# Summing 32,768 float32 rows into one: casting loads and a float16 fold, against float32 loads and a hand-written ring

## The chip, the cores and the metric

The kernel runs on one core of one Trainium2 chip. The metric is device time in microseconds (us) of one execution; of the kernel before, three runs gave a median of 629.18 us (629.15 to 629.20).

## The reference

```python
def reference(grad_output):            # [32, 1024, 2048] float32
    return np.sum(grad_output, axis=(0, 1)).astype(np.float32)
```

The input is 32,768 rows of 2048 float32 numbers, 268.4 MB. The result is the column sum: 2048 numbers, 8 KB. Every byte of the input has to come from HBM into the core's SBUF once.

## The kernel before, in words

The 32,768 rows are 256 "row blocks" of 128 rows, one row for each SBUF partition. A load takes m row blocks at a time: partition p gets m consecutive rows, so it reads m x 8 KB of consecutive bytes. A plan (a Python list, built before anything is recorded) names for each load the first row, m, the type it has in SBUF, the engine whose queue issues it, and the columns. In order:

- two loads of one row block each, kept as float32, issued on SP's queue (`PRE_TILES`);
- 30 loads of eight row blocks each (4 MB in SBUF), then one of four, two of two: issued on GpSimd's queue into float16 tiles, so that the transfer itself casts;
- five loads of one row block, float16;
- the last row block as four loads of 512 columns each, float16, last columns first.

All of it goes through one loop (lines 132 to 168). Line 146 issues the load. If the tile is float16 and has several rows a partition, VectorE adds its second half to its first in float16 (line 152), which halves what TensorE has to do. TensorE then multiplies a column of ones (the weights, `lhsT`, 128x1) with 512 columns at a time (line 161): the product is one row of 512 column sums over the 128 partitions, accumulated in one of four PSUM banks, `psum0` to `psum3`, one bank for each 512 columns. At the end ScalarE and VectorE copy two banks each to `res` (lines 175 and 177) and SP's queue writes `res` out (line 178).

The order of instructions is that of the loop; the tile framework puts in the waits. The eight-row tiles live in a pool of three buffers (`T_BUFS`), so a load waits until VectorE has added the tile three loads earlier.

Of the kernel before, what the change touches and what calls it, by code (L numbers as in the profile page):

```python
# [1 line left out]

# [4 lines left out]

P = 128
MM_N = 512  # L10

PRE_TILES = 2
PRE_M = 1
PRE_ENGS = ("sync", "sync")
BULK_M = 8
BULK_TAPER = (4, 2)
USE_DVE = True
TAIL_TILES = 5
COL_SPLIT_LAST = True
T_BUFS = 3  # L20
C_BUFS = 3
TAIL_BUFS = 8
BULK_ENGS = ("gpsimd",)
OUT_COPY_ENGS = ("scalar", "vector")


@with_exitstack
def kernel(
    ctx: ExitStack,
    tc: tile.TileContext,  # L30
    grad_output: bass.AP,
    out: bass.AP,
):
    nc = tc.nc
    fp32 = mybir.dt.float32
    fp16 = mybir.dt.float16

    D = out.shape[-1]
    flat = grad_output.rearrange("b s d -> (b s) d")
    R = flat.shape[0]  # L40
    assert R % P == 0 and D % MM_N == 0
    nbanks = D // MM_N
    n_row_blocks = R // P

    pre_tiles = min(PRE_TILES, n_row_blocks // PRE_M // 4)
    col_split = COL_SPLIT_LAST and nbanks > 1
    taper = [m for m in BULK_TAPER if m < BULK_M]
    n_small = TAIL_TILES + (1 if col_split else 0)
    while pre_tiles * PRE_M + sum(taper) + n_small > n_row_blocks:
        if TAIL_TILES and n_small > 1:  # L50
            n_small -= 1
        elif taper:
            taper = taper[1:]
        else:
            col_split = False
            n_small = min(n_small, 1)
            break
    n_tail = n_small - (1 if col_split else 0)

    plan: list = []  # L60
    row = 0
    for i in range(pre_tiles):
        plan.append((row, PRE_M, fp32, PRE_ENGS[i % len(PRE_ENGS)], 0, D))
        row += P * PRE_M
    tail_start = R - P * (n_small + sum(taper))
    bi = 0
    while row < tail_start:
        take = min(P * BULK_M, tail_start - row)
        plan.append((row, take // P, fp16, BULK_ENGS[bi % len(BULK_ENGS)], 0, D))
        bi += 1  # L70
        row += take
    for m in taper:
        plan.append((row, m, fp16, BULK_ENGS[bi % len(BULK_ENGS)], 0, D))
        bi += 1
        row += P * m
    for _ in range(n_tail):
        plan.append((row, 1, fp16, BULK_ENGS[bi % len(BULK_ENGS)], 0, D))
        bi += 1
        row += P
    if col_split:  # L80
        for b in range(nbanks - 1, -1, -1):
            plan.append((row, 1, fp16, BULK_ENGS[bi % len(BULK_ENGS)], b * MM_N, MM_N))
            bi += 1
        row += P
    assert row == R

    io_pool = ctx.enter_context(tc.tile_pool(name="io", bufs=T_BUFS))
    pre_pool = None
    if pre_tiles:
        pre_pool = ctx.enter_context(tc.tile_pool(name="pre", bufs=pre_tiles))  # L90
    c_pool = None
    if USE_DVE:
        c_pool = ctx.enter_context(tc.tile_pool(name="csum", bufs=C_BUFS))
    n_small_tiles = n_tail + (nbanks if col_split else 0)
    tail_pool = None
    if n_small_tiles:
        tail_pool = ctx.enter_context(
            tc.tile_pool(name="tail", bufs=min(n_small_tiles, TAIL_BUFS))
        )
    const_pool = ctx.enter_context(tc.tile_pool(name="const", bufs=1))  # L100
    psum_pool = ctx.enter_context(tc.tile_pool(name="psum", bufs=1, space=bass.MemoryType.PSUM))

    ones16 = const_pool.tile([P, 1], fp16)
    nc.vector.memset(ones16[:], 1.0)  # L104
    ones32 = None
    if pre_tiles:
        ones32 = const_pool.tile([P, 1], fp32)
        nc.vector.memset(ones32[:], 1.0)  # L108

    accs = [  # L110
        psum_pool.tile([1, MM_N], fp32, tag=f"psum{b}", name=f"psum{b}")
        for b in range(nbanks)
    ]
    res = const_pool.tile([1, D], fp32)

    def uses_dve(entry) -> bool:
        _, m, dt_, _, _, col_n = entry
        return USE_DVE and dt_ is fp16 and m > 1 and col_n == D

    def n_chunks(entry) -> int:  # L120
        _, m, dt_, _, _, col_n = entry
        n = (m * col_n) // MM_N
        return n // 2 if uses_dve(entry) else n

    total_mm = [0] * nbanks
    for e in plan:
        for j in range(n_chunks(e)):
            total_mm[((e[4] + j * MM_N) % D) // MM_N] += 1
    started = [False] * nbanks
    n_mm = [0] * nbanks  # L130

    for i, entry in enumerate(plan):
        row0, m, dt_, eng_name, col_lo, col_n = entry
        rows = flat[row0 : row0 + m * P]
        if col_n == D:
            src = rows.rearrange("(p m) d -> p (m d)", p=P)
        else:
            src = rows[:, col_lo : col_lo + col_n]

        if dt_ is fp16:  # L140
            big = m > 1 and col_n == D
            pool, tag = (io_pool, "T") if big else (tail_pool, "Ttail")
            T = pool.tile([P, m * col_n], fp16, tag=tag, name=f"t{i}")
        else:
            T = pre_pool.tile([P, m * col_n], fp32, tag="Tpre", name=f"t{i}")
        getattr(nc, eng_name).dma_start(out=T[:], in_=src)  # L146

        red = T
        if uses_dve(entry):
            half = (m * col_n) // 2  # L150
            C = c_pool.tile([P, half], fp16, tag="C", name=f"c{i}")
            nc.vector.tensor_tensor(  # L152
                out=C[:], in0=T[:, :half], in1=T[:, half:], op=mybir.AluOpType.add
            )
            red = C

        w = ones16 if dt_ is fp16 else ones32
        for j in range(n_chunks(entry)):
            b = ((col_lo + j * MM_N) % D) // MM_N
            n_mm[b] += 1  # L160
            nc.tensor.matmul(  # L161
                accs[b][:, :],
                lhsT=w[:],
                rhs=red[:, j * MM_N : (j + 1) * MM_N],
                start=(not started[b]),
                stop=(n_mm[b] == total_mm[b]),
            )
            started[b] = True

    bank_order = list(range(nbanks - 1, -1, -1)) if col_split else list(range(nbanks))  # L170
    for k, b in enumerate(bank_order):
        eng = OUT_COPY_ENGS[k % len(OUT_COPY_ENGS)]
        dst = res[:, b * MM_N : (b + 1) * MM_N]
        if eng == "scalar":
            nc.scalar.copy(out=dst, in_=accs[b][:, :])  # L175
        else:
            nc.vector.tensor_copy(out=dst, in_=accs[b][:, :])  # L177
    nc.sync.dma_start(out=out[None, :], in_=res[:])


# [1 line left out]
_INS = ['grad_output']  # L182
_OUTS = [((2048,), 'float32')]


# [23 lines left out]
```

## Time and profile before

| what | value |
|---|---|
| median of three runs | 629.18 us |
| span of the profiled execution, first to last instruction | 627.2 us |
| mean granted TensorE clock (1 is full speed) | 0.65 |
| casting loads of eight row blocks, 4096 KB each in SBUF | 30 |
| median time of one of them from issue to landing | 53.1 us |
| two float32 loads, 1024 KB each, issue to landing | 14.3 us |
| output, bytes | 8.0 KB |

The page counts the DMA's bytes and GB/s as they are written into SBUF; a casting load reads twice what it writes. "Busy" of an engine is the share of the span in which it runs an instruction; time in a queue or a wait is not counted. PE is TensorE's matmuls and PEld its weight loads, DVE is VectorE, ACT ScalarE, POOL GpSimd and SP the sync engine. A float32 matmul of the program appears as two records, and so do its weight loads: eight matmuls of the two float32 tiles are sixteen records. In the chain that ended last, "another core or an unknown queue" stands for a wait on a load that had been issued more than 50 us earlier. The time between the span and the run's time lies before the first and after the last instruction.

### The profile page before, as it was taken

The page shows a single profiled execution, that of the slowest core. Times are in us where ns is not written, and L with a number is a line of the kernel's source. Part 1 is how long each engine was busy: PE and PEld are TensorE (multiplying, and loading weights), DVE is VectorE, ACT ScalarE, POOL GpSimd, SP SyncE. Part 2 cuts the span into 40 slices and gives each one's busy share as a digit, 9 for nine tenths or more (in the row PEclk, how much of TensorE's full clock was granted, in tenths as well). Part 3 has the DMA queues.
Part 4 walks back from the last instruction along what each step waited for, and adds up shares of the span by engine and source line. Part 5 has one row for each costly group of instructions (what it writes and reads, how often), then busy time and mean ns, then how long its engine had stood idle before and what let it go on. Part 6 is the DMA issues. An engine that isn't in the chain of part 4 may idle for free.

```text
span 627.2 us, 1267 instructions
## 1 busy us (share of the span) xinstructions
PE 195.1 (31%) x536; PEld 58.1 (9%) x536; DVE 138.9 (22%) x37; ACT 2.4 (0%) x3; POOL 22.6 (4%) x46
## 2 busy tenths in 40 slices
PE   3323320333203333123341134321333312343165
PEld 0001100011000111001110011100111000111011
DVE  0202222022220122211222202222022221122320
ACT  0000000000000000000000000000000000000000
POOL 1000000000000000000000000000000000000110
PEclk9677556775567665667655776656676567665677
DMA  9999999999999999999999999999999999999997
GB/s 242 226 234 201 234 201 234 202 232 203 232 203 232 203 232 203 232 204 230 205 230 205 230 205 230 205 230 206 228 207 228 207 224 211 224 211 221 206 206 139
DMA packets 6344, 135.36 MB, mean 216 GB/s; under 512 B 705, under 2 KB 1217, under 8 KB 1857
## 3 DMA queue, kind: packets, MB, share of 16 engines
q0 software_dynamic: 6048, 133.17, 98.9%
q1 hardware_dynamic: 290, 2.11, 0.9%
q8 instruction: 4, 0.07, 0.0%
q14 instruction: 2, 0.02, 0.0%
HBM read 268.44 MB, written 0.01 MB: 428 GB/s over the span
## 4 chain that ended last, share of the span: by engine, by line
another core or an unknown queue 66%; DVE 21%; DMA 11%; PE 1%; POOL 1%; issue 0%; DVEq 0%; POOLq 0%
DVE c L152 20%; DMA t<-in_grad_output_dram 11%; PE psum L161 1%; POOL t L146 1%; DVEq L152 0%; DVE res L177 0%; POOLq L193 0%
## 5 line engine op out<-in xcount | busy, mean ns | idle before, releaser
L161 PE MATMUL psum<-c,ones 128*1 128x512 f16 x496 | 175.9, 533 | 405.5 <-DVE c L152 405.5
L152 DVE TENSOR_TENSOR c<-t 128x8192 f16<-128x8192 f16 (+2 forms) x33 | 137.5, 4167 | 471.1 <-DMA t<-in_grad_output_dram 471.1
L161 PEld LDWEIGHTS <-ones 128*1 128x1 f16 x520 | 56.5, 109 | 537.5 <-issue 516.4
L146 POOL DMA_DIRECT2D t<-in_grad_output_dram x42 | 22.4, 538 | 590.4 <-DVE c L152 575.3
L161 PE MATMUL psum<-t,ones 128*1 128x512 f16 (+1 forms) x40 | 19.4, 639 | 23.5 <-DMA t<-in_grad_output_dram 23.5
L177 DVE COPY res<-psum 1x512 f32<-1x512 f32 x2 | 1.4, 679 | 13.9 <-PE psum L161 13.9
L161 PEld LDWEIGHTS psum<-t,ones 128*1 128x1 f32 x16 | 1.6, 106 | 27.5 <-DMA t<-in_grad_output_dram 14.1
L175 ACT COPY res<-psum 1x512 f32<-1x512 f32 x2 | 1.1, 575 | 621.1 <-PE psum L161 621.1
L175 ACT ACT_TABLE_LOAD x1 | 1.3, 1283 | 0.7 <-PEq L193 0.7
L104 DVE MEMSET ones<- 128x1 f16 x1 | 0.1, 59 | 0.8 <-PEq L193 0.8
L193 POOL MEMSET const-float32-0.0<- 128x1 f32 x1 | 0.1, 100 | 0.2 <-issue 0.2
L193 POOL MEMSET const-bfloat16-1.0<- 128x1 bf16 x1 | 0.1, 103 | 0.0
L193 POOL MEMSET const-float32-1.0<- 128x1 f32 x1 | 0.1, 100 | 0.0
L193 POOL MEMSET const-uint8-127<- 128x1 uint8 x1 | 0.1, 100 | 0.0
L108 DVE MEMSET ones<- 128x1 f32 x1 | 0.1, 59 | 0.0
## 6 DMA issues: line engine op xcount, KB each, us to landing
t<-in_grad_output_dram POOLq DMA_DIRECT2D x30, 4096.0 KB, 53.1
t<-in_grad_output_dram POOLq DMA_DIRECT2D x5, 512.0 KB, 20.4
t<-in_grad_output_dram SPq DMA_DIRECT2D x2, 1024.0 KB, 14.3
t<-in_grad_output_dram POOLq DMA_DIRECT2D x2, 1024.0 KB, 26.6
t<-in_grad_output_dram POOLq DMA_DIRECT2D x1, 2048.0 KB, 29.0
t<-in_grad_output_dram POOLq DMA_DIRECT2D x4, 128.0 KB, 16.1
out_dram<-res SPq DMA_DIRECT2D x1, 8.0 KB
```

What stands on the lines that cost most here:

```text
L104: nc.vector.memset(ones16[:], 1.0)
L108: nc.vector.memset(ones32[:], 1.0)
L146: getattr(nc, eng_name).dma_start(out=T[:], in_=src)
L152: nc.vector.tensor_tensor(out=C[:], in0=T[:, :half], in1=T[:, half:], op=mybir.AluOpType.add)
L161: nc.tensor.matmul(accs[b][:, :], lhsT=w[:], rhs=red[:, j * MM_N : (j + 1) * MM_N], start=(not started[b]), stop=(n_mm[b] == total_mm[b]),)
L175: nc.scalar.copy(out=dst, in_=accs[b][:, :])
L177: nc.vector.tensor_copy(out=dst, in_=accs[b][:, :])
L193: nc = _bacc.Bacc("TRN2", target_bir_lowering=False, num_devices=1)
```

## The change

The kernel is written anew, with the waits set by hand (semaphores, `wait_ge`) in one block that the tile framework does not reorder.

- **Loads.** All loads are float32 and are issued on SP's queue. One buffer, `ring`, has three slots of eight rows a partition (3 x 64 KB a partition). 30 loads of eight row blocks go round the three slots; then come loads of 6, 4, 3 and 2 row blocks and the last row block in two pieces, columns 0 to 1663 and 1664 to 2047. Load i waits for `s_vec >= 2(i-2)`, that is for the first add of tile i-2, the last instruction that reads the slot.
- **VectorE.** The running sum is four rows a partition, 8192 numbers, held in the first half of the newest slot. For each load there are two float32 adds of 128x8192: the running sum of the slot before is added to the second half, then the second half to the first. Each add waits for the one before it by semaphore.
- **TensorE.** It does nothing until VectorE has finished the 30th tile. Then it sums the four running rows and the 16 late rows in float32, four matmuls of 512 columns for each row. The four go to four column groups of the array (`tile_position` 0, 32, 64, 96) and so to four partitions of a single PSUM bank.
- **End.** One copy by VectorE of that bank (128x512), one output DMA of four rows of 2 KB from partitions 0, 32, 64 and 96.

The core of the new code (`W` is 16384 numbers, a slot's width; `H` half of it; `Q` is 512):

```diff
-        getattr(nc, eng_name).dma_start(out=T[:], in_=src)
...
+        q = nc.sync
+        for i in range(VEC_TILES):
+            s = i % SLOTS
+            if i >= SLOTS:
+                q.wait_ge(s_vec, 2 * (i - 2))
+            src = flat[i * W // D * P : (i + 1) * W // D * P].rearrange("(p m) d -> p (m d)", p=P)
+            q.dma_start(out=ring[:, s * W : (s + 1) * W], in_=src).then_inc(landed[s], 16)
+        waited = 0
+        for k, (r0, m, c0, w, at) in enumerate(loads):
+            need = 2 * (VEC_TILES - 2) if (at + m * w - 1) // W == VEC_TILES % SLOTS else 2 * (VEC_TILES - 1)
+            if need > waited:
+                q.wait_ge(s_vec, need)
+                waited = need
...
+            q.dma_start(out=ring[:, at : at + m * w], in_=src).then_inc(late[k], 16)
...
-            nc.vector.tensor_tensor(
-                out=C[:], in0=T[:, :half], in1=T[:, half:], op=mybir.AluOpType.add
-            )
...
+        for i in range(VEC_TILES):
+            s = i % SLOTS
+            lo = ring[:, s * W : s * W + H]
+            hi = ring[:, s * W + H : (s + 1) * W]
+            v.wait_ge(landed[s], 16 * (i // SLOTS + 1))
+            if i:
+                b = ((i - 1) % SLOTS) * W
+                v.wait_ge(s_vec, 2 * i - 1)
+                v.tensor_tensor(out=hi, in0=hi, in1=ring[:, b : b + H], op=add).then_inc(s_vec, 1)
+                v.wait_ge(s_vec, 2 * i)
+            v.tensor_tensor(out=lo, in0=lo, in1=hi, op=add).then_inc(s_vec, 1)
...
+        def rows(at, w, c0, first, last):
+            for g in range(4):
+                lo, hi = max(c0, g * Q), min(c0 + w, (g + 1) * Q)
+                if lo >= hi:
+                    continue
+                yield t.matmul(
+                    acc[32 * g : 32 * g + 1, lo - g * Q : hi - g * Q],
+                    lhsT=ones[:],
+                    rhs=ring[:, at + lo - c0 : at + hi - c0],
+                    start=first,
+                    stop=last,
+                    tile_position=(0, 32 * g),
+                    skip_group_check=True,
+                )
+        t.wait_ge(s_one, 2)
+        t.wait_ge(s_vec, 2 * VEC_TILES - 1)
+        base = ((VEC_TILES - 1) % SLOTS) * W
+        for j in range(TILE_ROWS // 2):
+            for _ in rows(base + j * D, D, 0, j == 0, False):
+                pass
+        for k, (r0, m, c0, w, at) in enumerate(loads):
+            t.wait_ge(late[k], 16)
+            for j in range(m):
+                mm = list(rows(at + j * w, w, c0, False, k == len(loads) - 1))
+        mm[-1].then_inc(s_pe, 1)
...
+        a.wait_ge(s_pe, 1)
+        a.tensor_copy(out=res[:], in_=acc[:, :Q]).then_inc(s_res, 1)
+        q.wait_ge(s_res, 1)
+        q.dma_start(
+            out=out.rearrange("(g c) -> g c", g=4), in_=res[0:97:32, :]
+        ).then_inc(s_out, 16)
+        q.wait_ge(s_out, 16)
```

## The prediction

> **What bounds the kernel now.** I read the page's busy shares first, then the DMA queues, then the chain that ended last, and only then the groups of instructions.
>
> ```profile
> PE 195.1 (31%) x536; PEld 58.1 (9%) x536; DVE 138.9 (22%) x37; ACT 2.4 (0%) x3; POOL 22.6 (4%) x46
> ...
> DMA  9999999999999999999999999999999999999997
> ...
> q0 software_dynamic: 6048, 133.17, 98.9%
> q1 hardware_dynamic: 290, 2.11, 0.9%
> ...
> HBM read 268.44 MB, written 0.01 MB: 428 GB/s over the span
> ```
>
> No compute engine is busy for a third of the span, while the 16 DMA engines are full in all slices but the last. Queue q0 writes 133.17 MB because its loads turn float32 into float16; what it reads is twice that. In a stretch of the steady stage (100 to 293 us):
>
> ```profile
> DMA packets 1440, 41.91 MB, mean 217 GB/s; under 512 B 160, under 2 KB 160, under 8 KB 160
> ```
>
> 217 GB/s written is 434 GB/s read. The waits of VectorE give the same rate: its adds start at 66.06, 85.51 and 104.81 us, and the shortest step, 19.30 us, is one load of 8.39 MB read. So the kernel is a stream of 268.4 MB with a short head and a tail, and only what changes the stream's rate, its head or its tail counts. The end of the chain:
>
> ```profile
> 596.21 24.26 DMA t<-in_grad_output_dram
> 620.48 0.04 issue
> 620.52 3.59 PE psum L161 x8
> 624.10 0.02 issue
> 624.13 0.68 DVE res L177
> ```
>
> The reader is to see that the end hangs on the last loads, then on eight matmuls and one copy. The output DMA is issued at 624.90 and the span ends at 627.16, so it costs 2.26 us. The span is 2.0 us under the median of the runs (629.18); I keep these 2.0 us as a constant around it.
>
> **1. The stream: same bytes read, twice the bytes written.** All loads move from GpSimd's queue to SP's and land as float32. The question is whether a transfer that writes as much as it reads keeps 434 GB/s. The trace has one: the two first loads on q1, before q0 starts to move data (3 to 5.5 us):
>
> ```profile
> DMA packets 145, 1.06 MB, mean 423 GB/s; under 512 B 16, under 2 KB 16, under 8 KB 16
> ...
> q1 hardware_dynamic: 145, 1.06, 100.2%
> ```
>
> The engines are full and 423 GB/s are written and read. That is 2.5% under the 434 of q0, but these rows are 8 KB long, q0's rows are 64 KB. The loads of q0 that also have 8 KB rows (one row a partition) start their matmuls at 613.11, 615.58, 618.02 and 620.52 us: 2.47 us for 1.05 MB is 425 GB/s. So 8 KB rows give the same rate by either queue and with either width written; what differs is the row's length. The changed kernel loads 64 KB rows. Bounds: 268.4 MB at 423 GB/s is 634.5 us (every row as dear as an 8 KB row), at 19.30 us a load 32 x 19.30 = 617.6 us. I take 19.31, 618.0 us, from the rows of the same length, and 0.4 us for the last short pieces.
>
> **2. Do the loads stay back to back?** The new wait: load i waits on SP for the first add of tile i-2; behind it stand all later loads and the output DMA, and VectorE waits for those. That add starts when tile i-2 has landed and lasts some 8.7 us (below), while tile i-1 takes 19.3 us; load i is thus issued 10.6 us before it is needed. SP's issue took 0.40 us, and 1.9 us passed from its first issue (0.74) to steady packets. The cover is 10.6 - 2.3 = 8.3 us, so the wait costs nothing. GpSimd's 42 issues (22.4 us) vanish; they were hidden.
>
> **3. VectorE: two float32 adds of 8192 elements a load.** Not in the trace. The nearest rows:
>
> ```profile
> L152 DVE TENSOR_TENSOR c<-t 128x8192 f16<-128x8192 f16 x30 | 132.8, 4425 | 459.7 <-DMA t<-in_grad_output_dram 459.7
> ...
> L152 DVE TENSOR_TENSOR c<-t 128x2048 f16<-128x2048 f16 x2 | 2.5, 1226 | 3.0 <-DMA t<-in_grad_output_dram 3.0
> ...
> L177 DVE COPY res<-psum 1x512 f32<-1x512 f32 x2 | 1.4, 679 | 13.9 <-PE psum L161 13.9
> ```
>
> Float16: (4425 - 1226) / 6144 = 0.52 ns an element and 160 ns fixed. Bounds for float32: no dearer, 4.43 us; or the copy's whole 679 / 512 = 1.33 ns an element, 10.9 us. Taking the fixed 160 ns off the copy gives 1.01 ns, twice the float16 price, as twice the bytes would: 8.5 to 8.7 us. I take 8.7. Two adds, each with a semaphore step of 0.13 us (0.03 + 0.05 + 0.05 before an add in the chain), are 17.7 us a load, under the 19.3 of the load: hidden, 1.6 us to spare. The Trainium skill (VectorE: DVE Perf Modes, the section on the TRN2 errata) gives a float32 add of two tensors as (N + 151) / 0.96 ns, an estimate of 8.69 us here; no row of this trace shows it.
>
> **4. The last 16 rows, where the risk lies.** The 30th load lands at 2.45 + 0.25 + 30 x 19.31 = 582.0 us (head: step 5). VectorE's adds end at 599.7. Only then may TensorE start, on 4 running rows and on 16 late rows, of which six have already landed and the last lands at 621.1. A row of 2048 columns is four float32 matmuls. Their price:
>
> ```profile
> 27.57 0.13 PEld L161 LDWEIGHTS psum<-t,ones 128*1 128x1 f32 x1 [0.73 <-issue]
> 28.16 0.09 PEld L161 LDWEIGHTS psum<-t,ones 128*1 128x1 f32 x1 [0.47 <-issue]
> 28.59 0.08 PEld L161 LDWEIGHTS psum<-t,ones 128*1 128x1 f32 x1 [0.34 <-issue]
> 29.02 0.08 PEld L161 LDWEIGHTS psum<-t,ones 128*1 128x1 f32 x1 [0.34 <-issue]
> ```
>
> A matmul shows as two weight loads and two passes. A pass takes 0.43 us (28.59 to 29.02) once the clock is up and 0.855 us before (25.86 to 26.71); in this burst the clock came up after some 3 us. One after the other, a row is 8 x 0.43 = 3.44 us; with all four column groups side by side it is 0.86 us. Both ends: 20 rows cost 17.2 or 68.8 us, and some 2 us more for the cold start. TensorE has 621.1 - 599.7 = 21.4 us, so the overlap decides: at a mean of 0.97 us a row or less it waits for the loads, and the change costs nothing here. No row of the trace has two matmuls in different column groups. I take the overlap: each matmul here uses one column of the array ("128*1"), the groups have columns, weights and output partitions of their own, and the trace shows TensorE taking a second weight load (x2 at 25.05) before the first matmul has run. The Trainium skill speaks against it in part: TensorE: Matmul & The Clock Gate, Part 3, says that matmuls in different tiles run together but start and end in strict program order. As both passes of a matmul use one group, strict order lets the second pass of a group overlap only the first of the next; by that rule a row is four passes, an estimate of 1.72 us, and the sum would be the first rival's.
>
> **5. Head and tail.** Up to 2.76 us q1 had moved 0.13 MB, 0.31 us of work, so the stream starts in effect at 2.45 us. The changed kernel enters its hand-written part through one more barrier; nearest row: SP's 0.7 us wait at the start. Between 0 and 0.7 I take 0.25, and 0.2 at the exit (its row there: 0.6). Last landing: 2.45 + 0.25 + 618.0 + 0.4 = 621.1 us. Before, the last column pieces were still moving at 622.7, in the window from 613 at rates that fall to 25 GB/s. Then the last matmul, 384 of 512 columns, two passes: 0.65 us warm to 1.28 cold, I take 1.0; one copy of 512 columns, 0.68, with 0.03 and 0.09 around it; output 2.26; exit 0.2. 621.1 + 0.04 + 1.0 + 0.8 + 2.26 + 0.2 = 625.4 us, with the 2.0 around it **627.4 us**, 1.8 us less than before. By its own terms this case reaches from 625.7 (no barriers, warm, 19.30) to 628.8 (barriers at 0.7 and 0.6, cold, 1 us for short pieces).
>
> **Rivals.**
> - **Column groups overlap by pairs only** (slower). 20 x 1.72 + 2 = 36.4 us from 599.7: TensorE ends at 636.1, then 3.3 us: 639.4, **641.4 us**. For: two passes share a group. Against: nothing in the trace. It decides from about 0.97 us a row; an overlap of three gives 20 x 1.15 + 2 = 25 us, 630.0 us.
> - **No overlap at all**, the groups doing nothing: 599.7 + 70.8 = 670.5, **675.8 us**. For: every matmul in the trace runs alone.
> - **The stream pays for float32 writes or short packets**: up to 634.5 instead of 618.0 us, 642 at most, likelier 630 to 636. For: only 1.06 MB of such traffic is seen, and never beside a VectorE that is busy 90% of the time. Against: 423 beside 425.
> - **VectorE bounds**: from 9.5 us an add. At 10.9 a load takes 22.1 us, 2.8 more, thirty times: about 711 us. Against: the fixed part of the copy.
>
> **How the numbers follow.** A measurement of this kernel can tell about 0.2% (1.3 us) from no change; the bounds are 627.9 and 630.4 us. Forecast 0.52 (faster 0.43, same 0.09); pairs 0.17; no overlap 0.09; stream dearer 0.12 (same 0.03); overlap of about three 0.07 (faster 0.01, same 0.02); VectorE 0.03. Faster 0.44, same 0.14, slower 0.42. Faster and slower are about even, so the range takes in the pairs and the dearer stream and leaves out only no overlap and VectorE, and a little around: 625.7 to 642.5. The likeliest case's own range is 625.7 to 628.8.
>
> **What would show it.** Step 1: packets of 64 KB and some 434 GB/s on the hardware queue, and VectorE's first adds 19.3 us apart. Step 2: DMA at 9 in every slice but the last. Step 3: an add at 8.7 us, VectorE 85 to 90% busy. Step 4: matmuls of one row starting together, and TensorE idle before the last load; a TensorE that runs on after the last landing is a rival's. Step 5: output issued some 1.8 us after the last landing. The forecast is wrong if loads are over 19.4 us apart or TensorE ends over 2 us after them.

## The result, and the profile after

The changed kernel takes 630.87 us (median of 8 runs, 630.34 to 631.99), the kernel before on the same chip 629.05 us. The ratio is 1.0033 (95% interval 1.0023 to 1.0043): slower by a third of a percent. The time lies in the stated range, but on the other side of "no change" from the forecast.

The page of the changed kernel, first the busy shares, the DMA row and its queue:

```profile
span 629.2 us, 505 instructions
...
PE 20.0 (3%) x162; PEld 3.8 (1%) x162; DVE 514.0 (82%) x62; POOL 0.2 (0%) x4
...
DMA  9999999999999999999999999999999999999995
...
q1 hardware_dynamic: 5192, 268.45, 98.8%
...
L104 DVE TENSOR_TENSOR ring<-ring 128x8192 f32<-128x8192 f32 x29 | 252.1, 8692 | 65.8 <-DMA ring<-in_grad_output_dram 65.8
```

The DMA engines are still full in all slices but the last; VectorE went from 22% to 82% and still waits for loads, 65.8 us in all; its add takes 8692 ns. So the bound is the same stream. TensorE after VectorE's last add, from the timeline:

```profile
602.69 5.50 PE L118 MATMUL acc<-ring,ones 128*1 128x512 f32 x32 [602.69 <-DVE ring L106]
603.49 0.15 PEld L118 LDWEIGHTS acc<-ring,ones 128*1 128x1 f32 x4 [0.70 <-issue]
...
607.15 0.10 PEld L118 LDWEIGHTS acc<-ring,ones 128*1 128x1 f32 x4 [0.33 <-issue]
607.58 0.10 PEld L118 LDWEIGHTS acc<-ring,ones 128*1 128x1 f32 x4 [0.33 <-issue]
```

From 606.72 us on four weight loads appear every 0.43 us (some 0.85 us apart in the first four microseconds), where the kernel before had one: the four column groups run side by side, a row in 0.86 us. The end of the chain that ended last:

```profile
595.16 29.02 DMA ring<-in_grad_output_dram
624.18 0.04 issue
624.23 0.40 PE acc L118 x2
624.63 0.03 issue
624.66 0.88 PE acc L118 x2
625.53 0.02 issue
625.56 0.69 DVE res L143
```

The chain ends with a load, two short groups of matmuls and the copy. The output is issued at 626.27, and the span ends 2.93 us later. VectorE starts on the first and on the 30th tile here:

```profile
22.93 8.69 DVE L106 TENSOR_TENSOR ring<-ring 128x8192 f32<-128x8192 f32 x1 [21.27 <-DMA ring<-in_grad_output_dram]
...
585.12 8.69 DVE L104 TENSOR_TENSOR ring<-ring 128x8192 f32<-128x8192 f32 x1 [1.93 <-DMA ring<-in_grad_output_dram]
```

Against the prediction's steps:

| moment | predicted | measured |
|---|---|---|
| VectorE starts on the first tile (2.70 + 19.31) | 22.0 | 22.93 |
| VectorE starts on the 30th tile | 582.0 | 585.12 |
| last matmuls start, the last piece having landed | 621.1 | 624.66 |
| output issued | 622.9 | 626.27 |
| span's end | 625.4 | 629.2 |
| median (span and what lies around it) | 627.4 | 630.87 |

Of the 3.8 us missing in the span, 0.9 had gone by the first tile, 2.2 more by the 30th, 0.4 in the late loads, 0.5 behind the issue of the output; matmuls and copy took 0.2 less than assumed. Against the kernel before, the output is issued 1.4 us later (624.90 there), and 0.7 us more pass behind it (2.26 there). Around the span lay 1.8 instead of 2.0 us (the profiled run took 630.98 us).

### The profile page after: what moved, and what is told of

It is laid out like the page before. It is cut to its first block, busy times and chain, and to the rows that moved or that the text cites. A ratio compares the mean times of both kernels' runs of the same rounds, so it can differ in the third digit from the quotient of the medians.

```text
span 629.2 us, 505 instructions
## 1 busy us (share of the span) xinstructions
PE 20.0 (3%) x162; PEld 3.8 (1%) x162; DVE 514.0 (82%) x62; POOL 0.2 (0%) x4
## 4 chain that ended last, share of the span: by engine, by line
DMA 78%; DVE 21%; SPq 0%; PE 0%; issue 0%
DMA ring<-in_grad_output_dram 78%; DVE ring L104 21%; PE acc L118 0%; SPq L90 0%; DVE res L143 0%; SPq L78 0%; SPq L175 0%; SPq L50 0%
## 5 line engine op out<-in xcount | busy, mean ns | idle before, releaser
L104 DVE TENSOR_TENSOR ring<-ring 128x8192 f32<-128x8192 f32 x29 | 252.1, 8692 | 65.8 <-DMA ring<-in_grad_output_dram 65.8
L106 DVE TENSOR_TENSOR ring<-ring 128x8192 f32<-128x8192 f32 x30 | 260.7, 8692 | 22.3 <-DMA ring<-in_grad_output_dram 21.3
L118 PE MATMUL acc<-ring,ones 128*1 128x512 f32 (+1 forms) x162 | 20.0, 638 | 605.5 <-DVE ring L106 602.7
L118 PEld LDWEIGHTS acc<-ring,ones 128*1 128x1 f32 x162 | 3.8, 88 | 621.0 <-issue 615.0
```

Source lines behind the costliest of these rows:

```text
L104: v.tensor_tensor(out=hi, in0=hi, in1=ring[:, b : b + H], op=add).then_inc(s_vec, 1)
L106: v.tensor_tensor(out=lo, in0=lo, in1=hi, op=add).then_inc(s_vec, 1)
L118: yield t.matmul(acc[32 * g : 32 * g + 1, lo - g * Q : hi - g * Q], lhsT=ones[:], rhs=ring[:, at + lo - c0 : at + hi - c0], start=first, s ...
```

## The experiments

All are edits of the changed kernel, except b_warm, which edits the kernel before. The question is what took the 2.2 us between the tiles and the 1 us at the end. Theory A was VectorE's traffic in SBUF; its rivals were the queue, the place in memory, the width written, and single DMA engines that fall behind.

**a_again: nothing changed.**

> The changed kernel unchanged, for a second profile. What it tells apart: in the first profile the loads step by 19.32 us where nothing disturbs them (loads 10 to 13), by 19.35 from load 14 on, and by 19.37 to 19.58 in loads 3, 4, 5, 7, 8 and 9. If the place in memory sets this, the same loads are disturbed again by the same amounts. If it is chance (or something outside the kernel), the disturbed loads are others, and the sum of the 29 steps differs from 561.5 us by several tenths. Span expected 628.5 to 630.2 us either way.

Measured: 632.12 us in one run, span 630.3; VectorE's step from tile to tile is 19.388 us on average (19.386 in the first profile). Both profiles have one long step at tile 20, 20.12 and 19.98 us; the other longer steps are scattered in the first ten tiles, at other tiles in the two. The 19.32 us that the expectation gives for loads 10 to 13 is a misreading: those steps are 19.34 to 19.36 too, and the 29 steps of the first profile sum to 562.2 us, not 561.5. This span is 1.1 us longer at the very end: the last 23 matmul records took 4.51 us from 622.13 on, where the first profile had them done by 625.53. In these last microseconds the granted clock (third number from the right) was 0.50, and 1.00 in the first profile; a_again first:

```profile
622.80:626.20 3.40, 3.40 (x22) 0.69 (x14) 0.00 (x0) 0.00 (x0) 0.50 0.03 13
```

```profile
622.80:626.20 3.40, 2.61 (x26) 0.29 (x14) 0.64 (x1) 0.00 (x0) 1.00 0.04 17
```

Scatter and step 20 needed causes of their own.

**x_novec: VectorE nearly without work.** The sums are left out but for 64 of 8192 columns.

```diff
-            lo = ring[:, s * W : s * W + H]
-            hi = ring[:, s * W + H : (s + 1) * W]
+            lo = ring[:, s * W : s * W + 64]
+            hi = ring[:, s * W + H : s * W + H + 64]
...
-                v.tensor_tensor(out=hi, in0=hi, in1=ring[:, b : b + H], op=add).then_inc(s_vec, 1)
+                v.tensor_tensor(out=hi, in0=hi, in1=ring[:, b : b + 64], op=add).then_inc(s_vec, 1)
```

> VectorE's adds cut from 8192 to 64 columns, with every wait kept; this leaves out nearly all of the sums. Theory A (VectorE's traffic in SBUF slows the stream): the loads step by 19.32 us throughout, the 29 steps sum to 560.2 instead of 561.5 us, and the last landing comes some 1.3 us earlier. Theory B (the loads themselves, by queue or by memory): the steps stay at 19.35 on average with scattered longer ones, sum 561 to 562 us. As TensorE starts about 17 us earlier in both, the end moves only with the last landing: about 629.5 us by A, 630.9 us by B.

Measured: 630.86 us, ratio to the kernel before 1.0033 (1.0021 to 1.0045), the same as with all adds. An add now takes 225 ns; the steps still average 19.37 us, in this profile without scatter. Theory A falls: VectorE, at 82% of the span, costs the stream nothing that can be seen in the time.

**x_pool32: the same float32 loads on GpSimd's queue.**

```diff
-        q = nc.sync
+        q = nc.gpsimd
...
+        q = nc.sync
         q.wait_ge(s_res, 1)
```

> All float32 loads issued on GpSimd's queue instead of SP's; the output stays on SP's. If the hardware queue makes the loads uneven, they step as evenly as the casting loads did before (19.323 us each, 560.4 us for 29). If writing float32 does, they stay uneven (561 to 562 us). The head is longer in both: before, GpSimd's first packets started 5.5 us into the span against 1.8 on SP's queue, so I expect 2.5 to 3.7 us more from the head: 632 to 635 us.

Measured: 635.53 us, ratio 1.0101 (1.0084 to 1.0117), but the steps average 19.380 us, as on SP's queue: the queue is not what makes them longer. The head costs 0.9 us (first add at 23.80). My guess of 2.5 to 3.7 us for it was wrong. Most of the rest is at the exit, where 5.8 us pass from the output's issue (627.93) to the end of the span (633.7), 2.8 of them in SP's wait for GpSimd; y_drain takes that wait up. Another microsecond of this profile lies in the last matmuls, at a granted clock of 0.50 from 623.9 us on, as in a_again.

**x_rev: the tiles in reverse order.**

```diff
-            src = flat[i * W // D * P : (i + 1) * W // D * P].rearrange("(p m) d -> p (m d)", p=P)
+            r = VEC_TILES - 1 - i
+            src = flat[r * TILE_ROWS * P : (r + 1) * TILE_ROWS * P].rearrange("(p m) d -> p (m d)", p=P)
```

> The 30 eight-row tiles are loaded in reverse order of the rows; same work. If the place in memory makes the later loads step by 19.35 instead of 19.32 us (loads 14 to 29 in both profiles so far, and also with the loads on GpSimd's queue and with the adds cut short), loads 1 to 15 now step by 19.35 and the later ones by 19.32, with the scattered longer steps at the end. If the time since the start does, the pattern stays as it was.

Measured: 630.44 us in one run, steps 19.37 us on average and 19.34 to 19.36 from the second to the last but for one of 19.94 at tile 20. The stretch of 19.32 us that was to move did not exist, but the long step stayed at tile 20 with other rows in it, so the place in memory is not its cause. The scattered longer steps are missing here, as in x_novec, x_out1 and x_serial; they come in some profiles of the float32 loads and not in others.

**x_cast: casting loads in the hand-written form.** A ring of four float16 slots, loads on GpSimd's queue after two float32 rows on SP's, a float32 running sum in its own buffer, late rows as float16.

```diff
-    ring = sb.tile([P, SLOTS * TILE_ROWS * D], f32, name="ring")
+    ring = sb.tile([P, SLOTS * TILE_ROWS * D], f16, name="ring")
+    run = sb.tile([P, TILE_ROWS * D // 2], f32, name="run")
+    pre = sb.tile([P, PRE_ROWS * D], f32, name="pre")
...
+        q = nc.gpsimd
...
+            for h in range(2):
+                v.wait_ge(s_vec, 2 * i + h + 1)
+                half = ring[:, s * W + h * H : s * W + (h + 1) * H]
+                v.tensor_tensor(out=run[:], in0=run[:], in1=half, op=add).then_inc(s_vec, 1)
```

> The hand-written form with casting loads: two rows as float32 on SP's queue first, then 30 loads of eight rows into float16 on GpSimd's queue in a ring of four, a float32 running sum in a buffer of its own, late rows as float16. If writing float32 makes the loads step by 19.35 us, they step by 19.32 here as in the kernel before, 0.8 us less over 29 steps; if the hand-written structure does, by 19.35. The end as in the changed kernel (one copy, four output rows), the late rows one pass instead of two. Expected 628.5 us: 0.8 from the steps, 0.5 from the passes behind the last landing, some 1.0 from fewer transfers behind; by the other theory 629.5.

Measured: 631.92 us, ratio 1.0048 (1.0035 to 1.0062), slower, although the stream went as the width theory has it. The steps average 19.324 us, and there is no scatter (four of the nine float32 profiles have none either); the same stretch of VectorE's timeline, x_pool32 first, then x_cast:

```profile
198.03 8.69 DVE L104 TENSOR_TENSOR ring<-ring 128x8192 f32<-128x8192 f32 x1 [1.99 <-DMA ring<-in_grad_output_dram]
206.76 8.69 DVE L106 TENSOR_TENSOR ring<-ring 128x8192 f32<-128x8192 f32 x1
217.45 8.69 DVE L104 TENSOR_TENSOR ring<-ring 128x8192 f32<-128x8192 f32 x1 [2.00 <-DMA ring<-in_grad_output_dram]
226.18 8.69 DVE L106 TENSOR_TENSOR ring<-ring 128x8192 f32<-128x8192 f32 x1
236.81 8.69 DVE L104 TENSOR_TENSOR ring<-ring 128x8192 f32<-128x8192 f32 x1 [1.94 <-DMA ring<-in_grad_output_dram]
```

```profile
202.01 17.42 DVE L114 TENSOR_TENSOR run<-run,ring 128x8192 f32<-128x8192 f32 x2 [1.90 <-DMA ring<-in_grad_output_dram]
221.33 17.42 DVE L114 TENSOR_TENSOR run<-run,ring 128x8192 f32<-128x8192 f32 x2 [1.91 <-DMA ring<-in_grad_output_dram]
240.70 17.42 DVE L114 TENSOR_TENSOR run<-run,ring 128x8192 f32<-128x8192 f32 x2 [1.95 <-DMA ring<-in_grad_output_dram]
259.98 17.42 DVE L114 TENSOR_TENSOR run<-run,ring 128x8192 f32<-128x8192 f32 x2 [1.87 <-DMA ring<-in_grad_output_dram]
```

A tile starts where an idle time is shown in brackets: 198.03, 217.45, 236.81 (19.42 and 19.36) against 202.01, 221.33, 240.70, 259.98 (19.32, 19.37, 19.28). Same queue, adds of the same length: the float32 loads take longer. The scatter is not needed for it: the median step is 19.35 us in each of the nine float32 profiles and 19.32 in x_cast, y_drain, b_warm and the kernel before. The output was issued at 624.39, 1.9 us earlier than in the changed kernel, yet the span ended at 630.2. What SP waited for shows why:

```profile
SPq L55 <- POOLq L55: 2.8, 1, 2.8
SPq L55 <- DMA out_dram<-res: 1.1, 1, 1.1
```

At the exit of the hand-written block SP waits for the output and then 2.8 us more for GpSimd, whose drain there took 2996 ns.

**y_drain: the drain issued early.**

```diff
             q.dma_start(out=ring[:, at : at + m * w], in_=src).then_inc(late[k], 16)
+        q.drain()
```

> x_cast with one more drain on GpSimd right behind its last load. In x_cast the last bytes landed at 622.8 us and the output was issued at 624.4, earlier than in both kernels, but the span ended at 630.2: at the exit of the hand-written block GpSimd's drain took 3.0 us with everything waiting. In the kernel before the same engine drains from 612.7 us on, for 12.1 us, beside the last loads. If the drain's place makes the 3.0 us, it now runs beside the loads, the span ends at about 627.3 us and the median falls from 631.9 to about 629.0, level with the kernel before. If not, it stays at 631.9.

Measured: 629.22 us, ratio 1.0004 (0.9995 to 1.0013), 2.7 us less than x_cast. The drain moved to 569.4 us and ran for 55 us beside the loads:

```profile
L101 POOLq DRAIN  x1: 55233/55233/55233, 569.4 to 569.4; - x1
```

It beats the changed kernel (the intervals of the two ratios do not meet) and is level with the kernel before. From it to the changed kernel, which has the hand-written form with float32 loads, three slots and float32 late rows, is 1.65 us by the medians, and 1.9 us from output issue to output issue (624.36 and 626.27).

**x_code: more instructions on VectorE.**

```diff
             v.tensor_tensor(out=lo, in0=lo, in1=hi, op=add).then_inc(s_vec, 1)
+            for n in range(8):
+                v.memset(scr[:, 8 * i + n : 8 * i + n + 1], 0.0)
```

> Eight memsets of one column a tile are added on VectorE (240 short instructions; 0.5 us a tile, inside its 1.6 us of slack). In all profiles of the changed kernel one DMA engine falls behind the others by some 0.6 us at load 20, when 8 KB on the instruction queue are moved at 395 us, and never catches up. If instruction loading makes the lag, more and earlier transfers appear on the instruction queue and an engine falls behind at each of them, in the same load. If it is chance, the lag stays at load 20 or appears anywhere. Span 629 to 631 us.

Measured: 631.90 us in one run, span 630.1. The one 8 KB transfer of instructions became three, between 120 and 126, 350 and 358, and 568 and 574 us, and the long steps are there, each in the load during which instructions were moved. The line of the instruction queue, q14, reads the same in all three windows:

```profile
q14 instruction: 1, 0.01, 0.3%
```

```profile
119.75 8.69 DVE L105 TENSOR_TENSOR ring<-ring 128x8192 f32<-128x8192 f32 x1 [1.98 <-DMA ring<-in_grad_output_dram]
...
139.66 8.69 DVE L105 TENSOR_TENSOR ring<-ring 128x8192 f32<-128x8192 f32 x1 [2.37 <-DMA ring<-in_grad_output_dram]
```

```profile
352.52 8.69 DVE L105 TENSOR_TENSOR ring<-ring 128x8192 f32<-128x8192 f32 x1 [1.81 <-DMA ring<-in_grad_output_dram]
...
372.82 8.69 DVE L105 TENSOR_TENSOR ring<-ring 128x8192 f32<-128x8192 f32 x1 [2.76 <-DMA ring<-in_grad_output_dram]
```

The steps are 19.91 and 20.30 us, and the third, to 586.66, 20.33, against 19.35. A load signals in sixteen parts, and the trace has the time of each; I read a part as one DMA engine's share. At the three transfers the last part falls behind the median of its load by another 0.5, 1.0 and 1.0 us, and it never catches up: at the 30th tile the other fifteen are in 2.5 us before it. VectorE starts when the last part is in, so the output was issued at 627.19 instead of 626.27 us. In the changed kernel itself 8 KB are moved at 395 us and step 20 is 0.6 us too long; another 16 KB pass at 615 us, for 1.08 us, in the middle of the late rows. In x_novec the 8 KB come at 378 us, and the long step is 19, not 20. The kernel before has the same: 16 KB at 113.9 us, and its step from 104.81 to 125.10 is 20.3 instead of 19.3 us. A transfer need not show in a step: in x_cast 8 KB at 380 us set back a part that had been ahead, to just before the last, and the load came on time.

**x_serial: no column groups.** Four banks at partition 0.

```diff
-                    acc[32 * g : 32 * g + 1, lo - g * Q : hi - g * Q],
+                    acc[0:1, lo : hi],
...
-                    tile_position=(0, 32 * g),
```

> The same matmuls without column groups: four PSUM banks at partition 0, one copy of 1x2048, one output row. If the column groups are what makes four matmuls run in the time of one, a row costs eight passes of 0.43 us instead of two: 80 matmuls take 68.8 us plus 2 for the cold start from 602.7 us on, TensorE ends at about 673.5 and the span at about 679 us (the copy is 2.2 instead of 0.7 us). If matmuls on different PSUM banks run side by side without groups, the span stays near 631 us.

Measured: 680.61 us in one run, span 678.8. One weight load every 0.43 us at the end, and no pause for a load from 602.26 us on (the first line is the chain's):

```profile
602.26 71.66 PE acc L118 x162
```

```profile
671.59 2.31 PE L118 MATMUL acc<-ring,ones 128*1 128x512 f32 x7
672.02 0.08 PEld L118 LDWEIGHTS acc<-ring,ones 128*1 128x1 f32 x1 [0.34 <-issue]
672.45 0.08 PEld L118 LDWEIGHTS acc<-ring,ones 128*1 128x1 f32 x1 [0.34 <-issue]
...
673.94 2.28 DVE L142 COPY res<-acc 1x2048 f32<-1x2048 f32 x1 [71.83 <-PE acc L118]
```

The chain gives TensorE 71.66 us in one piece, against 20.0 us of busy time in the changed kernel. The groups are what keeps TensorE off the end.

**x_warm: TensorE kept busy in its pauses.**

```diff
+WARM = {1: 1, 2: 2}
...
+            for n in range(4 * WARM.get(k, 0)):
+                g = n % 4
+                t.matmul(
+                    spare[32 * g : 32 * g + 1, :],
+                    lhsT=ones[:],
+                    rhs=ring[:, at + g * Q : at + (g + 1) * Q],
...
```

> Twelve more matmuls into a spare PSUM bank fill TensorE's pauses after the four-row and the three-row load. Two profiles of the changed kernel end differently behind the last landing (624.2 us in both): 1.3 us of matmuls in the one, 2.5 in the other. If the clock's fall in the pauses makes this, the matmuls after the last landing take 0.9 to 1.3 us here, the runs above 631.5 us vanish and the median falls by some 0.5 us to about 630.4. If it is not the clock, the median stays at 630.9 or rises.

Measured: 630.73 us, ratio 1.0029 (1.0020 to 1.0039). In its profile the matmuls behind the last wait end as in the first profile, 1.3 us after it, and the longest run is 631.34 instead of 631.99; the median moved by 0.14 us, inside the interval. The clock explains single runs at most, not the loss: of the eight runs of the changed kernel the three at 631.60 us and above have a mean granted clock of 0.997, the other five 0.998 to 1.000, and all nine here 0.999 or 1.000.

**x_out1: the output as one row.** Three quarters of the output are zeros here.

```diff
-            out=out.rearrange("(g c) -> g c", g=4), in_=res[0:97:32, :]
+            out=out[None, :], in_=res[0:1, :]
```

> The output leaves as one row of 2048 from one partition, as in the kernel before, instead of four rows of 512 from four; three quarters of it are zeros here, since the sums of columns 512 to 2047 are not gathered. If the four rows cost the time between the issue of the output and the end (2.93 us against 2.26 before), the issue falls from 0.64 to 0.32 us, that time to some 2.4, and the median to about 630.4. If the barriers at the exit do, it stays at 2.9 and 630.9.

Measured: 630.39 us, ratio 1.0028 (1.0018 to 1.0039). The issue took 323 instead of 639 ns, and from the issue (625.61) to the end (628.2) it was 2.6 instead of 2.9 us, in the kernel before 2.26. So the four rows cost 0.3 us by the profile, while the times of the two kernels overlap. The 0.3 left are put down to the second barrier at the exit by elimination alone; this is not shown.

**b_warm: the kernel before with spare matmuls.**

```diff
+        if dt_ is fp16 and m == 1 and col_n == D:
+            for j in range(2):
+                nc.tensor.matmul(
+                    spare[:, :],
+                    lhsT=w[:],
+                    rhs=red[:, j * MM_N : (j + 1) * MM_N],
...
```

> The kernel before with two more matmuls into a spare PSUM bank after each single-row tile. There the last eight matmuls run at the low clock, 0.43 us each, from 620.52 to 624.10 us, though the last bytes land at 622.8. If the low clock is what ends last, TensorE ends at about 623.5 and the median falls by 0.5 to 0.6 us, to about 628.4; if the landing does, it stays at 629.0.

Measured: 628.53 us, ratio 0.9995 (0.9986 to 1.0003). TensorE now ends 0.39 us after its last wait, at 623.75, and the output is issued 0.35 us earlier, but that is no more than the measurement can tell. No version tried here beats the kernel before.

## Why the prediction was wrong

In the kernel before, VectorE starts on the tiles that point 1 is about here:

```profile
46.74 4.43 DVE L152 TENSOR_TENSOR c<-t 128x8192 f16<-128x8192 f16 x1 [14.90 <-DMA t<-in_grad_output_dram]
...
104.81 4.42 DVE L152 TENSOR_TENSOR c<-t 128x8192 f16<-128x8192 f16 x1 [14.87 <-DMA t<-in_grad_output_dram]
125.10 4.42 DVE L152 TENSOR_TENSOR c<-t 128x8192 f16<-128x8192 f16 x1 [15.87 <-DMA t<-in_grad_output_dram]
...
588.89 4.42 DVE L152 TENSOR_TENSOR c<-t 128x8192 f16<-128x8192 f16 x1 [14.94 <-DMA t<-in_grad_output_dram]
```

1. **The stream (step 1) failed in its size.** I took 19.31 us a load from the shortest steps at the start of the kernel before; measured were 19.39 us a load with float32 written, 2.2 us more over the 29 steps. The kernel before did not keep 19.31 us either. Its own mean from the second tile to the 30th was (588.89 - 46.74) / 28 = 19.36 us, and 32 loads of that are 619.6 instead of 618.0 us. The step to 125.10 us is 20.3 us; the prediction passed over it. That alone would have moved the forecast to 629.0, "no change". More than that, the sum was never put to the kernel before: 2.45 + 618.0 + 0.4 = 620.9 us, where step 5 itself notes that the last pieces were still moving at 622.7. The sum is 1.8 us short for the kernel before too, and 1.8 us was the whole gain forecast.
2. **"The same rate with either width written" held to about 0.3% and failed below that.** The rows showed 423 beside 425 GB/s; that comparison could not settle 0.3%, and the change is worth no more than that. With float32 written, a load steps by 19.36 to 19.39 us on average, by either queue, in either order of the rows, with VectorE busy or not (x_code's added transfers apart); with float16 written in the same form by 19.32 and 19.33. Over 29 steps that is 1.0 to 1.9 us, of which 0.4 to 0.8 us is the instruction transfer at step 20 (19 in x_novec) and, in the profiles that have it, up to 0.4 us the scatter. The quiet steps are 0.03 us longer, 0.8 us over 29. Why the wider write costs this is open, and so is the scatter. x_cast differs in slots and in the time of the issue too; the slots are an unlikely cause, as the kernel before also has three buffers and steps by 19.32 us.
3. **A term was missing: the slowest of 16 DMA engines.** The sum took all engines as equal, and a transfer as landed when its bytes were due. At the 30th tile of the changed kernel the median part landed 0.95 us before the last. An engine that loses 0.4 to 1 us to a transfer of instructions stays behind to the end; x_code shows the cause by adding such transfers. The kernel before pays nearly as much, 1.09 us at its 30th tile and 1.10 at its last load, against 1.53 at the last load of the changed kernel; so the term explains why the forecast was too early, and at most some 0.4 us of the loss between the two kernels. From the end of the last packet (624.24) to the matmul that waits for it (624.66) another 0.42 us pass, for which the sum had 0.04; at the first tile it is 0.34 us, from 22.57 to 22.91, of the 0.9 that had gone by then.
4. **The ring's wait (step 2), VectorE (step 3) and the entry barrier (step 5) were right.** DMA is at 9 in all slices but the last, an add takes 8.69 us (8.7 predicted; VectorE is busy 82% of the span, not 85 to 90%), SP's first issue came 0.2 us later (0.25 predicted).
5. **The column groups (step 4) were right**, and the estimate that spoke against them was not: from TensorE: Matmul & The Clock Gate (Part 3), a page of the Trainium skill, I had worked out that strict order would leave four passes a row, 1.72 us. The row takes two, 0.86 us, and x_serial shows eight for the same matmuls without groups. So float32 matmuls, which take two passes each, overlap fully across four groups. Whether this breaks the strict order, or the passes of the four groups alternate within it, is not shown: the records of the passes name no group.
6. **The output (step 5)** cost 2.93 instead of 2.46 us: 0.3 for four rows from four partitions, by x_out1's profile, the rest at the exit.
7. **Two bounds were added up wrongly.** The terms that the likeliest case names give 626.3 to 629.1 us, not 625.7 to 628.8, and the dearest stream 627.4 + 16.5 = 643.9, not 642.

The rival that came nearest is "the stream pays for float32 writes", which I had given 12% and priced at 630 to 636 us. None of the signs that were to show the forecast wrong appeared: the loads were 19.39 us apart (the sign was over 19.4), and TensorE ended 1.3 us after the last of them (the sign was over 2). They were too coarse for a gain of 0.3%.

## What to carry to other kernels

When a kernel is one stream and the change leaves its bytes alone, use the mean step of the whole stream, not a good one, and ask for the cause of every long step; then add a term for the slowest DMA engine. Put the sum to the kernel before first: what it misses there it will miss again. A gain of 0.3% worked out from rates that agree to 0.5% is not a forecast of a gain. At the end, count each hop from the last packet on: semaphore, matmul, copy, the rows of the output, and the drains and barriers behind it.

## What the runs showed that I had not expected

- Instructions are loaded by the same DMA engines as the data. After 8 KB of them the last part of each load came later for good, by 0.4 to 1.0 us with float32 loads and by 0 to 0.2 us in x_cast and y_drain, so a longer program can make the last landing later: with 240 more short instructions the output was issued 0.9 us later in the one profile of x_code.
- After GpSimd has issued loads, its drain at the exit of a hand-written block takes 3.0 us with everything waiting; issued early it runs beside the loads (12.1 us in the kernel before, 55 us in y_drain) and the median falls by 2.7 us (x_cast and y_drain).
- VectorE at 82% of the span, reading two float32 operands and writing one, took no measurable time from a DMA stream of 433 GB/s into the same memory (630.87 against 630.86 us).
